# Layer 0's attention mixers hold negated scores: the add-and-minimum of each row chunk gives the exponential's bias

## The chip, the cores and the metric

The kernel runs on one core of a Trainium2 chip. The metric is the time of one execution on the device in microseconds (us), the median over several runs; lower is better. A core has TensorE (PE, with the weight loads as PEld), VectorE (DVE), ScalarE (ACT), GpSimd (POOL) and SyncE (SP, which here issues the loads and stores), each with its own queue of instructions.

## The reference

A trunk of two layers over one sequence of 2048 tokens of width 1024, in float32. Layer 0 projects the normalised input once and runs two attention mixers side by side, each with 8 heads of 64 columns; their gated outputs go through one output projection. Layer 1 is a differential attention with its own projections.

```python
def sliding_window_sink_attention(q, k, v, sinks):        # mixer A
    # each chunk of 64 queries sees its own and the 2 chunks before
    scores = jnp.einsum('bcqhgd,bclhd->bchgql', qc, kb) / math.sqrt(HEAD_DIM)
    scores = jnp.where(valid, scores, NEG_INF)
    probs = jax.nn.softmax(jnp.concatenate([scores, sink], axis=-1), axis=-1)[..., :-1]
    out = jnp.einsum('bchgql,bclhd->bcqhgd', probs, vb)
...
def chunked_relbias_attention(q, k, v, rel_table):        # mixer B
    # each chunk of 64 queries sees its own and the 8 chunks before
    scores = jnp.einsum('bcqhd,bclhd->bhcql', qc, kb) / math.sqrt(HEAD_DIM)
    scores = scores + bias[None, :, None, :, :]           # learned, by clipped distance
    probs = jax.nn.softmax(jnp.where(valid, scores, NEG_INF), axis=-1)
    out = jnp.einsum('bhcql,bclhd->bcqhd', probs, vb)
```

A softmax is computed as exp(score - m) divided by its row's sum, where m is a number at least near the row's maximum. Mixer A's row has one more entry, the head's learned sink, which counts in the sum alone.

## The kernel before

Layer 0 first projects (names that begin with p0), stores queries, keys, values and gates to memory, and then `_mix0` runs the mixers (names that begin with m). Layer 1 follows (p1, then c).

In `_mix0` the tokens are handled in 4 blocks of 512, from the last block to the first. Each block has 8 A heads and 8 B heads, in pairs: two A heads, two B heads, and so on. A generator `heads` produces the scores of one head after the other (`scores_a`, `scores_b`) and puts its second half (`values_a`, `values_b`: transposes of the probabilities, products with the values, the join) into a queue; `pace` runs that queue 9 units behind the scores and lays the output projection (`mom`) or late gates (`mlg`) beside them. The order in which the instructions then stand on each engine is set by a scheduler when the program is built.

A score tile lies in one of 3 PSUM banks (tag S). One A head has 4 row chunks of 128 queries; two of them share a bank (`mSA`, 128 x 2 x 256). The kernel writes a large negative number over the masked corners (L633, L634; L632 in the first block of tokens), takes the maximum of each row with its sign turned (L635, result `manm`), takes the minimum of that and the negated sink (L637), and gives it to ScalarE as the exponential's bias (L641), which reads the bank and writes the probabilities to `mPA` in SBUF, of which there are 2 buffers. L642 computes the sink's share, L644 and L645 the row sums' reciprocal, and GpSimd multiplies (L647).

One B head has 4 row chunks of up to 640 keys, in two pieces of 384 and 256 (`mSB`), one bank each. L717 adds the mask or bias and takes the maximum in one custom operation, whose result is read by a second instruction (the accumulator read, `mbm`); it writes the sum to `mPB`, of which there are 8 buffers. L719 (or L721, where there is one piece) joins the two maxima and turns the sign (`mbnm`), L723 is the exponential, L724 the reciprocal `mbr` and L725 GpSimd's multiplication.

In the second halves TensorE transposes the probabilities into one of 3 banks (`mtrA` L675, `mtrB` L740), ACT and DVE split the result in a high and a low part (`mptH` L591, `mptL` L592), TensorE multiplies both by the values into one bank (`mOA`, `mOB`; L682, L684, L744, L745), and ACT and DVE join its halves (`mlow` L599, `myt` L600).

## Time and profile before

| | |
|---|---|
| median of 3 runs | 2830.96 us |
| lowest and highest run | 2825.42 and 2834.3 us |
| span of the profiled execution, first to last instruction | 2813.0 us |
| median less that span | 17.96 us |
| instructions | 44676 |
| layer 0's mixers, from the span's start | about 600 to 1130 us |

The profile records the span of one execution; what lies around it is known only as the difference to the median above. A row of the profile has the line of the source, the engine, the operation, what it writes and reads, shapes, the count, the busy time in us and the mean of one in ns, and then the engine's idle time before these instructions with what ended it. Matmuls overlap each other, so their means are longer than their pitch.

### The profile page before, as it was taken

What the parts mean: (1) busy time and instruction counts of PE and PEld (TensorE: products, weight loads), DVE (VectorE), ACT (ScalarE), POOL (GpSimd) and SP (SyncE); (2) the same over time, 40 slices, a digit from 0 to 9 for tenths busy, and PEclk for the clock granted to TensorE, in tenths of its full rate; (3) what the DMA queues carried; (4) which work ended last, traced back from release to release, by engine and by line L of the source; (5) the groups of instructions that cost most, each with busy time, mean ns of one, the idle gap of its engine ahead of it and who ended that gap; (6) DMA issues with size and microseconds to landing.
All of it is one profiled execution on the core that took longest, in us unless ns stands there. A gap on an engine that the chain in (4) does not pass through costs nothing.

```text
span 2813.0 us, 44676 instructions
## 1 busy us (share of the span) xinstructions
PE 2693.0 (96%) x13384; PEld 2164.3 (77%) x13384; DVE 1875.9 (67%) x5073; ACT 1623.8 (58%) x4135; POOL 1458.8 (52%) x1548
## 2 busy tenths in 40 slices
PE   7999999999899999889999999999999999999998
PEld 5888888888788888777788888776676777677776
DVE  7752285347788886598807880468786788777762
ACT  5443543267767675343435331578897787777761
POOL 3541252234645354266845660457676666767761
PEclk9999999999999999999999999999999999999999
DMA  5673343739977765565885444787868675455542
GB/s 174 223 244 138 109 142 121 221 111 240 234 191 189 199 186 140 184 239 194 252 268 187 128 142 142 238 253 208 238 199 234 181 215 186 140 175 152 168 148 85
DMA packets 356098, 521.73 MB, mean 185 GB/s; under 512 B 44816, under 2 KB 139792, under 8 KB 355856
## 3 DMA queue, kind: packets, MB, share of 16 engines
q1 hardware_dynamic: 355856, 518.87, 62.2%
q8 instruction: 107, 1.75, 0.3%
q14 instruction: 135, 1.11, 0.1%
HBM read 361.70 MB, written 157.02 MB: 184 GB/s over the span
## 4 chain that ended last, share of the span: by engine, by line
PE 72%; DVE 11%; DMA 8%; ACT 4%; issue 3%; POOL 1%; SPq 0%; DVEq 0%; ACTq 0%; POOLq 0%
PE cO L968 7%; PE p1mm L213 5%; PE p1mm L214 5%; PE p1mm L215 5%; PE cS L913 4%; PE cS L914 4%; PE ctr L964 3%; PE p0mm L213 3%; PE p0mm L214 3%; PE p0mm L215 3%; PE com L213 2%; PE com L214 2%; PE com L215 2%; PE mom L213 2%; PE mom L215 2%
## 5 line engine op out<-in xcount | busy, mean ns | idle before, releaser
L920 ACT ACTIVATE cP<-cS,cnm 128x512 f32<-128x512 f32 (+3 forms) x640 | 394.2, 622 | 121.7 <-DVE cnm L917 104.0
L917 DVE TENSOR_REDUCE cnm<-cS 128x1 f32<-128x512 f32 (+3 forms) x640 | 374.5, 601 | 52.9 <-PE cS L914 46.0
L952 POOL TENSOR_TENSOR cP<-cP,cP 128x512 f32<-128x512 f32 (+1 forms) x320 | 353.0, 1131 | 37.7 <-ACT cP L950 37.4
L951 POOL TENSOR_SCALAR cP<-cP,crl,cel 128x512 f32<-128x512 f32 (+3 forms) x288 | 209.4, 740 | 234.2 <-DVE crl L933 113.6
L213 PE MATMUL p1mm<-p1wH,p1hH 128*128 128x512 f32 x768 | 303.6, 396 | 5.5 <-ACT p1wH L308 5.5
L215 PE MATMUL p1mm<-p1wH,p1hL 128*128 128x512 f32 x768 | 304.0, 396 | 0.0
L214 PE MATMUL p1mm<-p1wL,p1hH 128*128 128x512 f32 x768 | 303.5, 396 | 0.1
L310 POOL TENSOR_TENSOR p0wL<-p0ws,p0wH 128x512 fp32r<-128x512 f32 (+1 forms) x124 | 149.8, 1237 | 265.6 <-ACT p0wH L308 255.2
L968 PE MATMUL cO<-cpt,cv 128*128 128x512 f32 (+3 forms) x640 | 285.4, 531 | 1.4 <-DVE cpt L966 1.3
L913 PE MATMUL cS<-ck,cqd 128*128 128x512 f32 (+3 forms) x640 | 264.2, 416 | 12.2 <-ACT cP L920 11.6
L966 DVE COPY cpt<-ctr 128x512 f32<-128x512 f32 (+1 forms) x320 | 191.4, 606 | 105.0 <-PE ctr L964 101.1
L213 PE MATMUL p0mm<-p0wH,p0hH 128*128 128x512 f32 (+1 forms) x640 | 238.4, 374 | 7.1 <-ACT p0vt L472 4.8
L215 PE MATMUL p0mm<-p0wH,p0hL 128*128 128x512 f32 (+1 forms) x640 | 238.4, 373 | 2.5 <-DVE p0hL L336 2.4
L214 PE MATMUL p0mm<-p0wL,p0hH 128*128 128x512 f32 (+1 forms) x640 | 238.6, 373 | 0.0
L310 POOL TENSOR_TENSOR p1wL<-p1ws,p1wH 128x512 fp32r<-128x512 f32 x128 | 167.8, 1331 | 127.9 <-ACT p1wH L308 121.3
L914 PE MATMUL cS<-ck,cql 128*128 128x512 f32 (+3 forms) x640 | 231.8, 366 | 0.0
L964 PEld LDWEIGHTS ctr<-ident,cP 128*128 128x128 f32 x1088 | 137.0, 141 | 115.4 <-issue 60.8
L950 ACT ACTIVATE cP<-cP,cc 128x512 f32<-128x512 f32 (+3 forms) x288 | 172.2, 662 | 15.7 <-DVE cc L948 15.3
L964 PE MATMUL ctr<-ident,cP 128*128 128x128 f32 x1088 | 175.2, 273 | 2.7 <-POOL cP L952 2.7
L213 PEld LDWEIGHTS p1mm<-p1wH,p1hH 128*128 128x128 f32 x768 | 145.7, 190 | 34.5 <-ACT p1wH L308 5.7
L214 PEld LDWEIGHTS p1mm<-p1wL,p1hH 128*128 128x128 f32 x768 | 145.5, 190 | 29.5 <-POOL p1wL L310 0.9
L215 PEld LDWEIGHTS p1mm<-p1wH,p1hL 128*128 128x128 f32 x768 | 145.4, 189 | 28.9
(303 smaller groups left out, 7115.9 us busy)
## 6 DMA issues: line engine op xcount, KB each, us to landing
p1ws<-in_od_w_in_dram SPq DMA_DIRECT2D x56, 512.0 KB, 4.2
p0ws<-in_ev_w_in_dram SPq DMA_DIRECT2D x48, 512.0 KB, 4.4
ck<-kH SPq DMA_DIRECT2D x144, 128.0 KB, 3.5
ck<-kL SPq DMA_DIRECT2D x144, 128.0 KB, 3.7
cv<-v SPq DMA_DIRECT2D x72, 256.0 KB, 4.2
cqd<-qH SPq DMA_DIRECT2D x128, 128.0 KB, 4.8
cql<-qL SPq DMA_DIRECT2D x128, 128.0 KB, 4.8
cwH<-wgH SPq DMA_DIRECT2D x64, 256.0 KB, 4.7
```

The costliest lines, as they stand in the source:

```text
L213: mm(ps, aH, bH, start=first, stop=False)
L214: mm(ps, aH, bL, start=False, stop=False)
L215: mm(ps, aL, bH, start=False, stop=last)
L310: low.tensor_tensor(l[:, :width], ws[:, k, :width], f32(h[:, :width]), ALU.subtract)
L913: mm(ps, qd[:, m, js], kt[:, :wd], start=True, stop=False)
L914: self.anchor = mm(ps, ql[:, m, js], kt[:, :wd], start=False, stop=True).ins
L917: nc.vector.tensor_reduce(nm[:, m, z:z + 1], ps, AX.X, ALU.max, negate=True)
L920: exp = nc.scalar.activation(chunks[z][:, :wd], ps, AF.Exp, bias=nm[:, m, z:z + 1], accum_out=acc).ins
L951: nc.gpsimd.tensor_scalar(p1, p1, rl[:, 0:1], e1, ALU.mult, ALU.mult)
L952: nc.gpsimd.tensor_tensor(p1, p1, p2, ALU.add)
L964: nc.tensor.transpose(tp[:, (j - j0) * P:(j - j0 + 1) * P], us[j][kt // 4][:, kk:kk + P], self.ident)
L968: mm(O[:, j0 * P:], v, T[:, :wd], start=(kt == 0), stop=(kt == nkt - 1), skip_group_check=True)
```

## The change

The query's scale is negative in layer 0 (`-0.125` in A's rotary table and in B's gain), so every score arrives negated, and the exponential is taken with scale -1 and the row's minimum as bias.

In mixer A the two memsets, the maximum and the sink's minimum are replaced by one custom operation for each row chunk (L636): it adds a mask tile `mwin` to the negated scores, writes the sum to `mPA`, and takes the minimum over the row, which starts from the negated sink. Its accumulator read gives `manm`. The exponential then works in place on `mPA` in SBUF. In the first block of tokens the half of the first row chunk that is masked as a whole is left out.

In mixer B the custom operation (L722) takes the minimum; the second piece of a row chunk starts from the first one's result, so the step that joined the two is gone. The reciprocal (L728) is taken for two row chunks at a time, and GpSimd's multiplications (L731) of the two follow it. `far` is no longer negated beforehand. The mask tile takes memory, and the scratch that the program keeps for DMA descriptors is made smaller (16384 to 1024 bytes of a partition).

```diff
+POS = -NEG
...
-        nc.vector.scalar_tensor_tensor(self.b_gain, gq, 0.125, gk, ALU.mult, ALU.mult)
+        nc.vector.scalar_tensor_tensor(self.b_gain, gq, -0.125, gk, ALU.mult, ALU.mult)
...
-                tabs["q"] = self.rope_tables(tb, self.gain[gq], 0.125, n + "tq")
+                tabs["q"] = self.rope_tables(tb, self.gain[gq], 0.125 if layer else -0.125, n + "tq")
...
+        win = ld.tile([P, 256], F32, tag="win", name=n + "win", bufs=1)
+        nc.gpsimd.memset(win, 0.0)
+        nc.gpsimd.memset(win[0:HD, 192:256], POS)
+        nc.gpsimd.memset(win[HD:P, 0:64], POS)
         nc.sync.dma_start(far, a["relfar"].to_broadcast([P, 8]))
-        nc.vector.tensor_scalar(far, far, -1.0, None, ALU.mult)
...
+            lows = [P if b * NTB + j == 0 else 0 for j in range(NTB)]
             for z in range(2):
...
-                if b == 0 and z == 0:
-                    nc.vector.memset(ps[:, 0, 0:P], NEG)
-                nc.vector.memset(ps[0:HD, :, 192:256], NEG)
-                nc.vector.memset(ps[HD:P, :, 0:64], NEG)
-                nc.vector.tensor_reduce(nm[:, zs], ps, AX.X, ALU.max, negate=True)
-                for j in (2 * z, 2 * z + 1):
-                    nc.vector.tensor_scalar(nm[:, j:j + 1], nm[:, j:j + 1], self.nsink[:, h:h + 1], None, ALU.min)
+                for i in range(2):
+                    j, lo = 2 * z + i, lows[2 * z + i]
+                    nc.vector.tensor_tensor_reduce(
+                        pt[:, j, lo:], ps[:, i, lo:], win[:, lo:], 1.0, self.nsink[:, h:h + 1], ALU.add, ALU.min, nm[:, j:j + 1]
+                    )
                 yield 1
                 for i in range(2):
-                    j = 2 * z + i
-                    nc.scalar.activation(pt[:, j, :], ps[:, i, :], AF.Exp, bias=nm[:, j:j + 1], accum_out=l[:, j:j + 1])
+                    j, lo = 2 * z + i, lows[2 * z + i]
+                    nc.scalar.activation(
+                        pt[:, j, lo:], pt[:, j, lo:], AF.Exp, bias=nm[:, j:j + 1], scale=-1.0, accum_out=l[:, j:j + 1]
+                    )
...
-            nc.gpsimd.tensor_scalar(bias, bias, 1.0, far[:, h:h + 1], ALU.mult, ALU.add)
-            nc.gpsimd.memset(bias[0:HD, 192:256], NEG)
+            nc.gpsimd.tensor_scalar(bias, bias, -1.0, far[:, h:h + 1], ALU.mult, ALU.add)
+            nc.gpsimd.memset(bias[0:HD, 192:256], POS)
+            l, r = small("bl", 4), small("br", 4)
...
-                    nc.vector.tensor_tensor_reduce(pb[:, ca:cz], ps, by, 1.0, NEG, ALU.add, ALU.max, m[:, z:z + 1])
-                if len(cuts) == 2:
-                    nc.vector.tensor_scalar(nm, m[:, 0:1], m[:, 1:2], -1.0, ALU.max, ALU.mult)
-                else:
-                    nc.vector.tensor_scalar(nm, m[:, 0:1], -1.0, None, ALU.mult)
+                    least = m[:, 0:1] if z else POS
+                    nc.vector.tensor_tensor_reduce(pb[:, ca:cz], ps, by, 1.0, least, ALU.add, ALU.min, m[:, z:z + 1])
                 yield 7 / 8
-                nc.scalar.activation(pb[:, w0:640], pb[:, w0:640], AF.Exp, bias=nm, accum_out=l)
-                nc.vector.reciprocal(r, l)
-                nc.gpsimd.tensor_scalar(pb[:, w0:640], pb[:, w0:640], r, 1.0, ALU.mult, ALU.mult)
+                nc.scalar.activation(
+                    pb[:, w0:640], pb[:, w0:640], AF.Exp, bias=m[:, z:z + 1], scale=-1.0, accum_out=l[:, j:j + 1]
+                )
+                if j % 2:
+                    nc.vector.reciprocal(r[:, j - 1:j + 1], l[:, j - 1:j + 1])
+                    for i in (j - 1, j):
+                        pi, wi = (probs[-1], max(0, 5 - t) * P) if i < j else (pb, w0)
+                        nc.gpsimd.tensor_scalar(pi[:, wi:640], pi[:, wi:640], r[:, i:i + 1], 1.0, ALU.mult, ALU.mult)
...
-    nc = bacc.Bacc("TRN2", target_bir_lowering=False, num_devices=1)
+    nc = bacc.Bacc("TRN2", target_bir_lowering=False, num_devices=1, dynamic_dma_scratch_size=1024)
```

The scheduler orders the instructions anew from the mixers' first score on. Up to there the order is the same, and so it is again in all of layer 1's mixer; in between each engine's order differs in many places.

On DVE, in the first block handled, where an A head's last scores and the next B head's first ones meet (ISA is the custom operation or its accumulator read), there stood before:

```order
L634 MEMSET mSA 64x2x64
L592 TENSOR_TENSOR mptL<-mtrB,mptH 128x128
L635 TENSOR_REDUCE manm<-mSA 128x2
L592 TENSOR_TENSOR mptL<-mtrB,mptH 128x384
L717 ISA mPB,mbm<-mSB,medge 128x384
L717 ISA mbm 128x1
L637 TENSOR_SCALAR manm<-manm,nsink 128x1 x2
L717 ISA mPB,mbm<-mSB,mbias 128x256
L717 ISA mbm 128x1
L592 TENSOR_TENSOR mptL<-mtrB,mptH 128x256
L592 TENSOR_TENSOR mptL<-mtrB,mptH 128x128
L719 TENSOR_SCALAR mbnm<-mbm 128x1
```

On DVE at the same place there stands now:

```order
L596 TENSOR_TENSOR mptL<-mtrB,mptH 128x256
L596 TENSOR_TENSOR mptL<-mtrB,mptH 128x128
L636 ISA mPA,manm<-mSA,mwin,nsink 128x256
L636 ISA manm 128x1
L636 ISA mPA,manm<-mSA,mwin,nsink 128x256
L636 ISA manm 128x1
L722 ISA mPB,mbm<-mSB,medge 128x384
L722 ISA mbm 128x1
L596 TENSOR_TENSOR mptL<-mtrB,mptH 128x384
L722 ISA mPB,mbm<-mSB,mbias,mbm 128x256
L722 ISA mbm 128x1
```

A bank of mixer A is done after two operations and their reads, which now write `mPA`; the splits that lay between the steps of the maximum stand ahead of them or behind; mixer B's second operation reads the first one's result.

On TensorE, in the second block handled, from the last transpose of an A head whose `mPA` the second A head of the next pair uses, there stood before:

```order
L675 MATMUL mtrA<-ident,mPA 128x128
L215 MATMUL mom<-mw,myL 128x512
L585 MATMUL mSB<-mks,mqd 128x384
L586 MATMUL mSB<-mks,mql 128x384
L740 MATMUL mtrB<-ident,mPB 128x128 x8
L682 MATMUL mOA<-mptH,mvA 128x128
L684 MATMUL mOA<-mptL,mvA 128x128
```

On TensorE at the same place there stands now:

```order
L678 MATMUL mtrA<-ident,mPA 128x128
L215 MATMUL mom<-mw,myH 128x512
L216 MATMUL mom<-mw,myL 128x512
L214 MATMUL mom<-mw,myH 128x512
L215 MATMUL mom<-mw,myH 128x512
L216 MATMUL mom<-mw,myL 128x512
L589 MATMUL mSB<-mks,mqd 128x384
L590 MATMUL mSB<-mks,mql 128x384
L746 MATMUL mtrB<-ident,mPB 128x128 x4
L589 MATMUL mSB<-mks,mqd 128x256
L590 MATMUL mSB<-mks,mql 128x256
L214 MATMUL mom<-mw,myH 128x512
```

The B head's second score (128x256) needs the bank that the A head's first two minimums free, and these wait for the transpose at the top; more of the output projection moved in between.

On TensorE, at such a transpose in the first block handled, there stood before:

```order
L675 MATMUL mtrA<-ident,mPA 128x128
L585 MATMUL mSB<-mks,mqd 128x384
L586 MATMUL mSB<-mks,mql 128x384
L740 MATMUL mtrB<-ident,mPB 128x128 x8
L585 MATMUL mSB<-mks,mqd 128x256
L586 MATMUL mSB<-mks,mql 128x256
L213 MATMUL mlg<-p0hH,p0wH 128x512
```

On TensorE at the same transpose there stands now:

```order
L678 MATMUL mtrA<-ident,mPA 128x128
L216 MATMUL mlg<-p0hH,p0wL 128x512
L589 MATMUL mSB<-mks,mqd 128x384
L590 MATMUL mSB<-mks,mql 128x384
L746 MATMUL mtrB<-ident,mPB 128x128 x4
L589 MATMUL mSB<-mks,mqd 128x256
L590 MATMUL mSB<-mks,mql 128x256
L589 MATMUL mSB<-mks,mqd 128x384
L590 MATMUL mSB<-mks,mql 128x384
L746 MATMUL mtrB<-ident,mPB 128x128 x4
```

Here two scores follow one another closely behind the transpose, each in a bank that two of the A head's minimums free.

More of the change, by code (lines that the diff above doesn't have):

```diff
@@ L564, in _mix0 @@
         nc.gpsimd.memset(edge, 0.0)
-        nc.gpsimd.memset(edge[HD:P, 0:64], NEG)
+        nc.gpsimd.memset(edge[HD:P, 0:64], POS)
+        win = ld.tile([P, 256], F32, tag="win", name=n + "win", bufs=1)
+        nc.gpsimd.memset(win, 0.0)
+        nc.gpsimd.memset(win[0:HD, 192:256], POS)
+        nc.gpsimd.memset(win[HD:P, 0:64], POS)
         nc.sync.dma_start(far, a["relfar"].to_broadcast([P, 8]))
-        nc.vector.tensor_scalar(far, far, -1.0, None, ALU.mult)
         group = {}
@@ L622, in scores_a @@
             pt = sb.tile([P, NTB, 256], F32, tag="PA", name=n + "PA")
+            lows = [P if b * NTB + j == 0 else 0 for j in range(NTB)]
             for z in range(2):
-                zs = slice(2 * z, 2 * z + 2)
                 ps = pS.tile([P, 2, 256], F32, tag="S", name=n + "SA")
@@ L628, in scores_a @@
                     c0 = (b * NTB + j - 1) * P - k0
-                    lo = P if c0 < 0 else 0
-                    score(ps[:, i, lo:256], res["q"], j, ks, c0 + lo, c0 + 256)
-                if b == 0 and z == 0:
-                    nc.vector.memset(ps[:, 0, 0:P], NEG)
-                nc.vector.memset(ps[0:HD, :, 192:256], NEG)
-                nc.vector.memset(ps[HD:P, :, 0:64], NEG)
-                nc.vector.tensor_reduce(nm[:, zs], ps, AX.X, ALU.max, negate=True)
-                for j in (2 * z, 2 * z + 1):
-                    nc.vector.tensor_scalar(nm[:, j:j + 1], nm[:, j:j + 1], self.nsink[:, h:h + 1], None, ALU.min)
+                    score(ps[:, i, lows[j]:256], res["q"], j, ks, c0 + lows[j], c0 + 256)
+                for i in range(2):
[3 more added lines that the diff above has]
+                    )
                 yield 1
                 for i in range(2):
-                    j = 2 * z + i
-                    nc.scalar.activation(pt[:, j, :], ps[:, i, :], AF.Exp, bias=nm[:, j:j + 1], accum_out=l[:, j:j + 1])
+                    j, lo = 2 * z + i, lows[2 * z + i]
+                    nc.scalar.activation(
+                        pt[:, j, lo:], pt[:, j, lo:], AF.Exp, bias=nm[:, j:j + 1], scale=-1.0, accum_out=l[:, j:j + 1]
+                    )
             nc.scalar.activation(es_, nm, AF.Exp, bias=self.sink[:, h:h + 1])
@@ L646, in scores_a @@
             for j in range(NTB):
-                nc.gpsimd.tensor_scalar(pt[:, j, :], pt[:, j, :], r[:, j:j + 1], 1.0, ALU.mult, ALU.mult)
+                nc.gpsimd.tensor_scalar(pt[:, j, lows[j]:], pt[:, j, lows[j]:], r[:, j:j + 1], 1.0, ALU.mult, ALU.mult)
             res.update(p=pt, v=vt, k0=k0)
@@ L711, in scores_b @@
                 cuts = [(w0, 384), (384, 640)] if w0 < 384 else [(w0, 640)]
-                m, nm, l, r = small("bm", 2), small("bnm"), small("bl"), small("br")
+                m = small("bm", 2)
                 for z, (ca, cz) in enumerate(cuts):
```

## The prediction

> **What bounds the kernel now.** I read the page first, then a table of stretches, then what TensorE waits for in the stretch that the change touches, then the groups of instructions with shapes apart.
>
> ```profile
> span 2813.0 us, 44676 instructions
> PE 2693.0 (96%) x13384; PEld 2164.3 (77%) x13384; DVE 1875.9 (67%) x5073; ACT 1623.8 (58%) x4135; POOL 1458.8 (52%) x1548
> PE 72%; DVE 11%; DMA 8%; ACT 4%; issue 3%; POOL 1%; SPq 0%; DVEq 0%; ACTq 0%; POOLq 0%
> ```
>
> TensorE is busy for 96% of the span and carries 72% of the chain that ended last; DVE is the next owner with 11%. No TensorE instruction is removed, so only TensorE's idle time can be won. The stretches, in microseconds from the span's start, say how much of it lies where layer 0's two mixers run:
>
> ```profile
> core 0: us, PE busy (x) PEld busy (x) DVE busy (x) ACT busy (x) POOL busy (x), PEclk, DMA share, GB/s
> 540.00:600.00 60.00, 58.75 (x257) 47.68 (x256) 7.16 (x11) 21.00 (x35) 13.31 (x14) 1.00 0.51 151
> 600.00:1130.00 530.00, 496.61 (x3097) 437.63 (x3096) 412.14 (x1529) 369.07 (x987) 259.36 (x389) 0.99 0.74 192
> 1130.00:1200.00 70.00, 61.84 (x287) 50.53 (x286) 39.78 (x73) 25.29 (x58) 15.52 (x11) 0.95 0.65 207
> 1200.00:2813.00 1613.00, 1563.10 (x7175) 1198.39 (x7174) 1109.21 (x2781) 971.11 (x2504) 977.41 (x950) 0.99 0.63 190
> ```
>
> The mixers of layer 0 fill 600 to 1130: 530 us, of which TensorE is idle for 530.00 - 496.61 = 33.4. DVE is busy for 412 of them (78%), and the DMA engines for 74%. After 1200 layer 1 runs; the order of its mixer is not changed on any engine, so I leave it at its time. What ends TensorE's idle time in 600 to 1130, in total, times and longest:
>
> ```profile
> PE mtrB L740 <- DVE mptL L592: 8.8, 13, 2.2
> PE mOB L744 <- DVE myt L600: 4.7, 10, 0.8
> PE mSA L585 <- ACT mPA L641: 3.0, 2, 2.2
> PE mSB L586 <- DMA mql<-bqL: 3.0, 3, 1.3
> PE mSB L585 <- ACT mPA L641: 2.9, 6, 1.0
> PE mom L215 <- POOL myL L612: 2.5, 1, 2.5
> PE mSB L585 <- DVE mbm L717: 2.0, 3, 0.7
> PE mSB L585 <- ACT maes L642: 1.6, 1, 1.6
> PE mOA L682 <- DVE myt L600: 1.3, 2, 0.9
> PE mtrA L675 <- DVE mptL L592: 1.1, 2, 0.8
> ```
>
> Two kinds matter. A score that waits for mixer A's exponential (L641, L642) waits for a score bank: 3.0 + 2.9 + 1.6 = 7.5 us. A wait for DVE is one for a split, a join or a minimum that stood in DVE's queue: 8.8 + 4.7 + 2.0 + 1.3 + 1.1 = 17.9 us. DMA (3.0) and GpSimd (2.5) own the rest. A third loss sits inside the busy time:
>
> ```profile
> 698.73:702.14 3.41, 3.41 (x13) 2.99 (x12) 2.56 (x13) 1.62 (x4) 0.00 (x0) 0.51 1.04 208
> 733.00:736.27 3.27, 1.38 (x5) 0.64 (x5) 2.20 (x5) 3.22 (x9) 3.27 (x7) 0.99 0.80 110
> 736.27:739.68 3.41, 3.02 (x10) 2.62 (x10) 2.48 (x9) 2.98 (x8) 3.41 (x7) 0.51 1.01 355
> 770.41:773.82 3.41, 3.41 (x15) 3.08 (x15) 3.29 (x8) 2.15 (x5) 2.57 (x7) 0.51 0.85 215
> 896.70:900.11 3.41, 1.06 (x7) 0.51 (x4) 3.38 (x8) 3.08 (x11) 2.47 (x3) 0.99 1.04 274
> 900.11:903.52 3.41, 3.37 (x17) 3.37 (x18) 1.93 (x6) 3.02 (x12) 1.95 (x5) 0.51 1.06 237
> ```
>
> The columns are those above. When TensorE was busy for only 1.38 or 1.06 us of some 3.3, the next 3.41 us ran at half the granted clock, which costs about 3.41/2 = 1.7 us. With the windows from 698.73 and 770.41 there are four in this stretch, 6.8 us. The Trainium skill, "TensorE: Matmul & The Clock Gate", section "HAM oscillation — how this bites in real kernels", gives the rule as no idle gaps above about 3.4 us; by it, stalls of at most 2.5 us would leave the clock alone and this term would be zero. The trace disagrees, and the trace decides.
>
> **The change part by part.** The rows that price it:
>
> ```profile
> L641 ACT ACTIVATE mPA<-mSA,manm 128x256 f32<-128x256 f32 x128 | 59.6, 475 | 20.3 <-DVE manm L637 18.6 <-PE mSA L586 1.3 <-PE mlg L215 0.2
> L641 ACT ACTIVATION_READ_ACCUMULATOR mPA<-mSA,manm 128x1 f32 x128 | 26.4, 206 | 0.0
> L717 DVE CUSTOM_DVE_ANT_0 mPB<-mSB,mbias 128x256 f32<-128x256 f32 x120 | 50.1, 417 | 7.9 <-PE mSB L586 5.0 <-PE mtrB L740 2.3
> L717 DVE DVE_READ_ACCUMULATOR2_ANT mbm<- 128x1 f32 x240 | 19.7, 82 | 0.0
> L635 DVE TENSOR_REDUCE manm<-mSA 128x2 f32<-128x512 f32 x64 | 43.0, 676 | 0.8
> L633 DVE MEMSET mSA<- 64x128 f32 x64 | 10.5, 165 | 11.0 <-PE mSA L586 6.6
> L634 DVE MEMSET mSA<- 64x128 f32 x64 | 10.5, 165 | 5.9
> L637 DVE TENSOR_SCALAR manm<-manm,nsink 128x1 f32<-128x1 f32 x128 | 18.9, 193 | 0.2
> L719 DVE TENSOR_SCALAR mbnm<-mbm 128x1 f32<-128x1 f32 x112 | 22.8, 205 | 0.1
> L721 DVE TENSOR_SCALAR mbnm<-mbm 128x1 f32<-128x1 f32 x16 | 2.4, 148 | 0.2
> L724 DVE RECIPROCAL mbr<-mbl 128x1 f32<-128x1 f32 x128 | 20.4, 159 | 18.1 <-ACT mPB L723 16.2 <-POOL mPB L725 0.9
> L723 ACT ACTIVATE mPB<-mPB,mbnm 128x256 f32<-128x256 f32 x8 | 4.0, 502 | 2.0 <-DVE mbnm L721 1.2 <-POOL myt L605 0.8
> ```
>
> Mixer A, DVE. Out go the memsets, the maximum and the sink's minimum: 10.5 + 10.5 + 43.0 + 18.9 = 82.9 us. In come 128 add-and-minimums of 128x256 with their accumulator reads, the form of L717: 128 x (417 + 82) = 63.9 us. Their first value is a column in memory, where L717 has a constant. No row prices that; the nearest is a one-column operation with a column operand (L719, 205 ns) against one without (L721, 148), 57 ns, so 128 x 57 = 7.3 us, between 0 and 128 x 205 = 26.2. Net -11.7.
>
> Mixer B, DVE. Out go the negated maxima, 22.8 + 2.4 = 25.2 us, and half of the reciprocals, since one of two columns serves two chunks: 10.2. The second minimum now takes the first one's result as a column: 112 x 57 = 6.4 us, and waits for it; the bounds are 0 and 112 x 205 = 23.0. Net -29.0. Together DVE gets 40.7 us lighter, 412 to 371, with bounds of -54 and -5 (both columns at 0 and at 205 ns).
>
> That does not itself move the end. I turn it into waits by DVE's free time: 530 - 412 = 118 us before and 159 after. The load over the free time falls from 3.5 to 2.3, by a third, and I let the 17.9 us of waits for DVE fall as much: -6.0. Bounds 0 (the waits are dependencies through ACT and not queueing) and -17.9.
>
> Mixer A's score banks. A bank is free today after memsets, maximum and sink's minimums (2 x 165 + 676 + 2 x 193 = 1392 ns) and two exponentials (2 x 475 = 950), at least 2.3 us; after the change the exponential reads memory and the bank is free after two minimums, 2 x 499 = 1.0 us. I keep 43% of the 7.5 us: -4.3. Bounds 0 and -7.5.
>
> The clock. Two of the four half-speed windows should go with the shorter stalls: -3.4. Bounds 0 and -6.8.
>
> The exponential of A, ACT. It reads SBUF in place of PSUM: 502 ns against 475, 128 x 27 = 3.5 us on an engine that is busy for 369 of 530 us and that TensorE waits for through the banks, which are now free before it: 0. The Trainium skill, "Perfetto Trace Analysis", section "Optimizing Scalar/DVE Operations", speaks against this move: about 93 ns of access per ScalarE instruction on SBUF against 51 on PSUM. By it 128 x 42 = 5.4 us is my estimate, hidden in the same place; the row's smaller difference is used.
>
> Normalisation of B in pairs, GpSimd. The same multiplications, the even one a chunk later, the odd one behind it. GpSimd is busy for 259 of 530 us, and TensorE waits for no normalisation in the list above: 0. If that cover failed, it would be one multiplication per pair. The masks (two more memsets and a tile, once), the negated far bias, the signs in the rotary tables and the gain, and the first block's half-width tiles are single instructions before 600 or shorter ones off the path: 0. The smaller DMA scratch only frees memory; every load is issued by SP in both: 0.
>
> **The new wait.** Mixer A's minimum now writes the probability tile, of which there are two, so it must wait until TensorE has transposed the head two before. Today only the exponential writes there. One second head of a pair:
>
> ```profile
> 724.66 0.69 DVE L635 TENSOR_REDUCE manm<-mSA 128x2 f32<-128x512 f32 x1
> 727.76 0.28 PE L675 MATMUL mtrA<-ident,mPA 128*128 128x128 f32 x1
> ```
>
> The maximum ran at 724.66, and the last transpose of the tile that its head will use ended at 728.04: a minimum in its place would have stood for 3.4 us, and behind it in DVE's queue the splits and joins that TensorE needs. The order of the changed kernel shows what TensorE has to do meanwhile. In the second block, 11 TensorE instructions lie between that transpose and the first score that needs the freed bank, and 16 before the next one; at 496.61/3097 = 0.160 us each that is 1.8 and 2.6 us, against 1.0 and 2.0 us for two and four minimums. There it is covered. In the first block handled one pair has 7 and 9 of them: 1.1 and 1.4 us against 1.0 and 2.0, a wait of 0.56 us. Counted in the same way over all pairs of the changed order, seven second heads have 4 to 7 and 9 to 11 instructions, and the rest have about enough; 7 x 0.56 = 3.9 us of new wait. Bounds 0 and the first rival's price.
>
> The sum: -6.0 - 4.3 - 3.4 + 3.9 = -9.8 us, a span of 2803.2. The median of the three runs, 2830.96, lies 17.96 above the profiled span; I take that as what lies around the span and unchanged, so 2830.96 - 9.8 = 2821.2, stated as 2821.
>
> **The rivals.**
> First, slower: the new wait decides. Sixteen pairs of A heads run, and 14 or 15 second heads reuse a tile that was busy late; I count 14. If half of the 3.4 us reached TensorE at each, that is 14 x 1.7 = 24 us in place of 3.9, and with the gains of 13.7 the time is 2830.96 + 10.3 = 2841. It decides from 13.7/14 = 0.98 us per pair. For it: the row at 724.66, and that DVE's queue is strict. Against it: the order puts some of TensorE's other work behind the transpose at every pair.
> Second, the same: what goes from DVE comes back as another wait. The DMA engines are at 1.01 to 1.06 in the windows above, so heads that finish sooner may only wait for their loads, which the waits for mql (3.0) already show; and the DVE waits may be chains through ACT. Then the banks and the new wait alone count, -4.3 + 3.9, and the time is 2831.
> Third, the change does more: all three terms at their bounds, -17.9 - 7.5 - 6.8 = -32, which gives 2799. Against it: a join costs its chain through ACT however free DVE is.
>
> **How the numbers follow.** A change of 0.3%, 8.5 us, is about what a measurement of this kernel tells from none. The forecast gets 0.52, and since its sum of 9.8 is only just beyond that bound, 0.37 of it lies on the faster side and 0.15 on the side of no change; its own range is 2812 to 2828. The third rival has 0.09, the second 0.26 and the first 0.13. That makes 0.46 for faster, 0.41 for no change and 0.13 for slower. The range for 8 in 10 takes in the second rival and reaches into the first and the third: 2804 to 2838.
>
> **What would show it.** Between 600 and the end of the mixers, TensorE's idle time falls from 33 to some 27 us and DVE's busy time by about 41; the scores' waits for L641's successor vanish and a smaller one for the minimum stands in their place; half-speed windows fall from four to two; layer 1's length stays. The forecast is wrong if DVE shows idle time at A's minimum that ends with a transpose and TensorE's waits for splits and joins grow with it, or if waits for loads take over.

## The result, and the profile after

| | before | after |
|---|---|---|
| median of 15 runs each | 2826.11 us | 2814.32 us |
| lowest and highest run | 2819.56 and 2834.3 us | 2810.95 and 2825.77 us |
| ratio of after to before, 95% interval | | 0.9965 [0.9953, 0.9976] |
| span of the profiled execution | 2813.0 us | 2810.4 us |

The ratio is worth 2826.11 x 0.0035 = 9.9 us (the medians themselves lie 11.8 apart); 9.8 had been forecast. In the last group of experiments the same pair gave 0.9961 [0.9947, 0.9975], 11 us. The page of after, the lines that answer to the first ones of before:

```profile
span 2810.4 us, 44478 instructions
PE 2699.2 (96%) x13384; PEld 2168.2 (77%) x13384; DVE 1838.0 (65%) x4808; ACT 1629.7 (58%) x4135; POOL 1456.0 (52%) x1551
PE 77%; DVE 8%; DMA 7%; ACT 3%; issue 2%; POOL 1%; SPq 1%; DVEq 0%; ACTq 0%; POOLq 0%
```

DVE's share of the chain fell from 11% to 8%, TensorE's rose to 77%. The spans differ by only 2.6 us, far less than the medians: the execution of before that was profiled was a short one, and one execution cannot carry the comparison. So I cut both kernels from A's first score to layer 1's first transposes, the stretch that the change touches, and use two executions of each: of before the first profile and that of a kernel with the same order of instructions (the first experiment below), of after the first profile and a repeat. The columns are those of the stretches in the prediction. Before, twice:

```profile
600.70:1148.10 547.40, 511.50 (x3161) 449.58 (x3160) 418.76 (x1547) 374.01 (x999) 259.95 (x389) 0.99 0.75 194
```

```profile
596.30:1149.60 553.30, 515.97 (x3161) 453.02 (x3160) 421.59 (x1547) 373.75 (x999) 260.08 (x389) 0.98 0.74 192
```

After, twice:

```profile
595.90:1139.10 543.20, 514.05 (x3162) 449.52 (x3161) 385.32 (x1283) 377.90 (x999) 259.32 (x389) 0.98 0.71 195
```

```profile
600.10:1139.60 539.50, 509.28 (x3161) 446.34 (x3160) 386.15 (x1283) 377.94 (x999) 259.37 (x389) 0.99 0.71 197
```

The stretch is 550.4 us on average before and 541.4 after, 9.0 less, beside the 9.9 of the ratio. TensorE's idle time (length less the first busy column) was 35.9 and 37.3, and is 29.2 and 30.2; its busy time, with the same matmuls, was 511.5 and 516.0 and is 514.1 and 509.3. What follows the stretch lasted 1664.9 and 1674.7 us before, 1671.3 and 1682.7 after (span less the stretch's end). These lie 18 us apart for a layer whose mixer stands in one order, and they do not follow the kernel: in the experiments below, too, they run from 1668.6 to 1681.2. So I take them as differences between executions, and not as the change's. What TensorE waits for after, between 600 and 1130:

```profile
PE mtrB L746 <- DVE mptL L596: 12.9, 26, 1.6
PE mOB L750 <- DVE myt L604: 5.3, 13, 0.8
PE mSB L589 <- DVE manm L636: 1.9, 4, 0.7
PE mSB L590 <- DMA mql<-bqL: 1.2, 2, 1.0
PE mtrA L678 <- DVE mptL L596: 0.7, 1, 0.7
```

The scores' waits for A's exponential (7.5 us) are gone, with 1.9 us for the new minimum in their place; the waits of B's scores for the maximum that frees their bank (L717, 2.0) are gone too. The waits for splits did not shrink as forecast but grew, from 8.8 to 12.9. The rows that price the new instructions, shapes apart:

```profile
L722 DVE CUSTOM_DVE_ANT_0 mPB<-mSB,mbias,mbm 128x256 f32<-128x256 f32 x112 | 53.4, 477 | 4.3 <-PE mSB L590 2.5
L636 DVE CUSTOM_DVE_ANT_0 mPA<-mSA,mwin,nsink 128x256 f32<-128x256 f32 x120 | 52.3, 479 | 13.1 <-PE mtrA L678 5.6 <-PE mSA L590 3.4 <-DMA g<-p0gt 2.3
L728 DVE RECIPROCAL mbr<-mbl 128x2 f32<-128x2 f32 x64 | 10.4, 162 | 13.5 <-ACT mPB L724 12.8
L642 ACT ACTIVATE mPA<-mPA,manm 128x256 f32<-128x256 f32 x120 | 59.6, 499 | 6.6 <-DVE manm L636 6.4
```

And what DVE waits for in the stretch: one row of before (its first profile), then two of after.

```profile
DVE mptL L592 <- ACT mptH L591: 21.4, 36, 4.4
```

```profile
DVE mptL L596 <- ACT mptH L595: 38.8, 46, 4.4
DVE mPA L636 <- PE mtrA L678: 6.2, 6, 2.1
```

The last row is the new wait: six times A's minimum stood until TensorE had transposed the head two before. The rows above it fit the splits that did not come sooner: DVE waited 21.4 us for ScalarE's half of a split in the first profile of before (24.2 in the second), and waits 38.8 (36.9) now. A lighter DVE that arrives earlier and waits for ScalarE would look like this; that ScalarE is not later instead was not tested.

### The profile page after: what moved, and what is told of

Its sections match the earlier page's. It is cut to its first block, busy times and chain, and to the rows that moved or that the text cites. A ratio compares the mean times of both kernels' runs of the same rounds, so it can differ in the third digit from the quotient of the medians.

```text
span 2810.4 us, 44478 instructions
## 1 busy us (share of the span) xinstructions
PE 2699.2 (96%) x13384; PEld 2168.2 (77%) x13384; DVE 1838.0 (65%) x4808; ACT 1629.7 (58%) x4135; POOL 1456.0 (52%) x1551
## 4 chain that ended last, share of the span: by engine, by line
PE 77%; DVE 8%; DMA 7%; ACT 3%; issue 2%; POOL 1%; SPq 1%; DVEq 0%; ACTq 0%; POOLq 0%
PE cO L974 7%; PE p1mm L216 5%; PE p1mm L214 5%; PE p1mm L215 5%; PE cS L919 4%; PE p0mm L214 4%; PE cS L920 4%; PE p0mm L215 4%; PE p0mm L216 4%; PE ctr L970 3%; PE com L214 2%; PE mom L214 2%; PE com L215 2%; PE com L216 2%; PE mom L215 2%
## 5 line engine op out<-in xcount | busy, mean ns | idle before, releaser
L958 POOL TENSOR_TENSOR cP<-cP,cP 128x512 f32<-128x512 f32 (+1 forms) x320 | 353.0, 1130 | 38.0 <-ACT cP L956 37.6
L215 PEld LDWEIGHTS p1mm<-p1wL,p1hH 128*128 128x128 f32 x768 | 146.0, 190 | 29.9 <-POOL p1wL L311 0.9
```

The source lines that it names most:

```text
L215: mm(ps, aH, bL, start=False, stop=False)
L958: nc.gpsimd.tensor_tensor(p1, p1, p2, ALU.add)
```

## Experiments

Each kernel was timed beside the kernel before on its chip; the three groups of four ran on three chips. All changed kernels but the first are ordered anew by the scheduler, so that an edit is never quite alone; where that weakens a reading I say so. The stretch is that of the tables above, of one execution each; half-speed windows are of 3.41 us, inside it.

| kernel | ratio to before, 95% | stretch, us | TensorE idle | half-speed windows |
|---|---|---|---|---|
| before | 1 | 547.4 | 35.9 | 4 |
| same order, smaller scratch | 1.0000 [0.9983, 1.0017] | 553.3 | 37.3 | 7 |
| A alone | 1.0025 [1.0009, 1.0042] | 558.9 | 36.9 | 9 |
| A alone, three mPA | 0.9993 [0.9977, 1.0009] | 551.2 | 37.4 | 6 |
| B: pairs of reciprocals alone | 0.9995 [0.9978, 1.0012] | 552.1 | 37.1 | 7 |
| B: chained minimum alone | 0.9966 [0.9946, 0.9986] | 544.0 | 35.2 | 4 |
| B alone | 0.9948 [0.9930, 0.9965] | 542.7 | 32.2 | 4 |
| B alone, again | 0.9960 [0.9945, 0.9975] | 541.4 | 30.5 | 4 |
| after | 0.9965 [0.9953, 0.9976] | 543.2 | 29.2 | 5 |
| after, again | 0.9961 [0.9947, 0.9975] | 539.5 | 30.2 | 2 |
| after, three mPA | 0.9946 [0.9926, 0.9966] | 542.0 | 29.9 | 5 |
| after, work added in the projection | 0.9988 [0.9970, 1.0006] | 544.8 | 32.6 | 3 |
| after, work added behind A's minima | 1.0032 [1.0014, 1.0050] | 560.9 | 41.9 | 7 |
| after, A's banks held longer | 0.9993 [0.9981, 1.0006] | 549.8 | 35.9 | 8 |

**The scratch size alone.** The kernel before with the last line of the diff.

```
-    nc = bacc.Bacc("TRN2", target_bir_lowering=False, num_devices=1)
+    nc = bacc.Bacc("TRN2", target_bir_lowering=False, num_devices=1, dynamic_dma_scratch_size=1024)
```

> The kernel before with only the smaller DMA scratch (1024 bytes of a partition); every engine's order is that of the kernel before. Theory (the gain of 10 us comes from layer 0's mixers): no difference, ratio to the kernel before 0.999 to 1.001. Rival (the scratch or another placement in memory brings the gain): 0.9965. Its profile is also a second look at the old order: if the mixers' stretch, from the first score of mixer A to the first transpose of layer 1's projection, is again 547 us, executions of one program agree there; if it is 550 or more, the first profile was a fast execution.

2826.48 us, ratio 1.0000 [0.9983, 1.0017]: the scratch is worth nothing that can be measured. Since every engine's order is that of before, its profile also served as a second one of before, and it showed how far executions of one order differ: 11.3 us in the span, 5.9 in the stretch (547.4 and 553.3), so that the first one was a fast one, as the expectation had it for 550 or more.

**Mixer A's part alone.** A's lines of the diff (win, the add-and-minimum, the exponential on mPA, the half-width tiles and the sign of the query's table); B as before.

> Mixer A changed, mixer B as before (its gain positive, maxima joined, one reciprocal for each chunk). Theory (TensorE's waits for score banks held by mixer A's exponential went away, 7.5 us to about 2): most of the gain, -5 to -8 us, ratio 0.997 to 0.998, with no wait of a score for L642 in the list. Rival (a lighter DVE is what counts, and B sheds 29 of the 41 us): -3 us, 0.999. Rival (the new order as a whole is luck): any value, and the parts don't add up.

2835.53 us, ratio 1.0025 [1.0009, 1.0042]: slower, where the theory and the rival of the lighter DVE both had a gain. The stretch, what TensorE waited for in it, and DVE's row for the new wait:

```profile
598.60:1157.50 558.90, 522.05 (x3162) 455.32 (x3161) 402.67 (x1475) 379.14 (x999) 259.44 (x389) 0.97 0.73 190
```

```profile
PE mSB L590 <- DVE manm L637: 6.7, 6, 3.2
PE mSB L591 <- DMA mql<-bqL: 6.2, 4, 4.4
PE mSB L590 <- DMA mqd<-bqH: 2.3, 2, 2.1
```

```profile
DVE mPA L637 <- PE mtrA L679: 7.3, 9, 1.8
```

DVE is busy for 16 to 19 us less (402.7 against 418.8 and 421.6), and TensorE idles as long as before, 36.9 us. The waits for banks that the exponential held are gone; the minimum's own (6.7) and those for queries (6.2 + 2.3) have their place, in stalls of up to 4.4 us. What is longer in this execution is TensorE's busy time (522.05 against 511.5 and 516.0), with nine half-speed windows. It was a long execution of its kernel (2840.6 us), so the trace does not say how the 8 us of the medians come about.

**Mixer B's part alone.** B's lines of the diff (the chained minimum, the sign of the gain, the bias and the edge, reciprocals in pairs); A as before.

> Mixer B changed, mixer A as before. Theory of the banks: the scores' waits for A's exponential stay at 6 to 9 us, and the gain is small, 0 to -3 us, ratio 0.999 to 1.000. Rival (lighter DVE): -7 us, 0.9975.

2813.11 us, ratio 0.9948 [0.9930, 0.9965]: all of the gain, and more than either expectation had. A's banks are held as before, and that still shows:

```profile
596.50:1139.20 542.70, 510.54 (x3161) 448.28 (x3160) 405.66 (x1354) 375.21 (x999) 260.28 (x389) 0.99 0.71 195
```

```profile
PE mtrB L743 <- DVE mptL L592: 8.1, 14, 2.8
PE mSB L585 <- ACT mPA L641: 4.8, 7, 1.7
PE mSA L585 <- ACT mPA L641: 2.4, 2, 2.2
```

Against the two profiles of before, the waits of B's scores for the maximum went from 2.0 and 2.0 to 0.8, those of the output projection for GpSimd (L612) from 2.5 and 2.7 to nothing, and those for queries from 3.0 and 5.7 to 1.1 + 1.1 = 2.2. So only 1.2 us of the gain lie in scores' waits for the operation that B's part changes.

DVE's busy column is only 13 to 16 us lower, less than with A alone. This does not show that B's part takes less off DVE, since the column counts overlapping records once (in the first execution of before the records add up to 503.9 us, where it has 418.8). By its own rows B's part sheds 22.8 + 2.4 us of joins and 20.4 - 10.4 of reciprocals and adds 112 x 60 ns = 6.7, which is 28.5 less; A's part sheds 19.6, as worked out below. After these two runs the amount of DVE's work and its place are both still possible. The parts could also simply add up: 1.0025 x 0.9948 = 0.9973 lies inside the interval of the whole change.

**A third buffer for mPA in the changed kernel.**

```
-            pt = sb.tile([P, NTB, 256], F32, tag="PA", name=n + "PA")
+            pt = sb.tile([P, NTB, 256], F32, tag="PA", name=n + "PA", bufs=3)
```

> The changed kernel with three buffers of mPA in place of two, so that mixer A's minimum need not wait for the transposes of the head two before. Theory (the new wait costs a few us of TensorE, 1.9 shown as waits for the minimum and part of the grown waits for splits): 2 to 5 us faster than the changed kernel, ratio 0.995 to 0.996 to the kernel before, and DVE's idle time at the minimum that ends with a transpose (6.2 us) gone. Rival (that wait is covered): as the changed kernel, 0.9965.

2813.59 us, ratio 0.9946 [0.9926, 0.9966]. DVE's wait for the transposes of `mtrA` is gone from its list, and the time is that of B alone. The ratios of this kernel and of the whole change differ by 2826 x 0.0019 = 5 us, and their intervals overlap, so the new wait may cost some us in the whole change, or nothing. TensorE's list has one long row beside this:

```profile
PE mSB L590 <- DMA mql<-bqL: 6.5, 5, 2.5
```

Waits for queries of 6.5 us, more than in either profile of before, thus stand in a kernel that is as fast as any here.

**A third buffer with A alone.** The same line in the kernel with A's part alone.

> The kernel before with the change made in mixer A alone, and a third buffer for A's probabilities mPA. Theory W (A alone is slower because its minimum, which now writes mPA, waits for the transposes that last read that buffer: 7.3 us of waits of DVE in the run of A alone, and 7.1 us of TensorE behind it): the wait goes, and with it most of the 8 us; 2822 to 2829, ratio 0.998 to 1.001. Rival L (A's loss comes from its longer instructions on ScalarE and DVE, and from the order that the scheduler makes of them): 2832 to 2838, ratio 1.002 to 1.004.

2827.25 us, ratio 0.9993 [0.9977, 1.0009], as theory W had it: without the wait for the transposes A alone costs nothing that can be measured, and brings nothing either. The stretch, and what TensorE's list has now:

```profile
602.80:1154.00 551.20, 513.79 (x3162) 451.14 (x3161) 400.92 (x1475) 379.68 (x999) 259.33 (x389) 0.98 0.73 193
```

```profile
PE mSB L591 <- DMA mql<-bqL: 7.3, 5, 3.6
PE mSA L591 <- DMA mql<-aqL: 4.1, 1, 4.1
PE mSB L590 <- DMA mqd<-bqH: 1.5, 1, 1.5
PE mSB L590 <- DVE manm L637: 0.2, 1, 0.2
```

The minimum's 6.7 us are down to 0.2, and the waits for queries stand at 7.3 + 4.1 + 1.5 = 12.9 us, against 3.0 in the first profile of before and 5.7 in the second. TensorE's idle time is the same with two buffers and with three (36.9 and 37.4 us); the shorter stretch lies in its busy time (522.05 and 513.79), with six half-speed windows in place of nine. The two kernels with A alone ran on different chips, each beside the kernel before. That the waits for queries took what the lighter DVE could have brought fits these rows; the kernel above, fast with 6.5 us of them, speaks against it, and no run tested it.

**Work added to DVE, at a place that the scheduler chose.** After, with a reduction of a constant table per score bank of A.

```
+                nc.vector.tensor_reduce(small("load"), edge, AX.X, ALU.min)
```

> The changed kernel with one more reduction of a 128x384 table on DVE behind A's minima of each score bank (64 of them, results unused): it puts some 25 to 30 us back on DVE, and leaves all waits and buffers as they are. Theory D (the prediction's first term: TensorE's waits for DVE shrink with DVE's work): the gain shrinks by two thirds; 2820 to 2826, ratio 0.998 to 1.000. Rival C (what counts is the work between a score and its exponential in B, not DVE's sum; a lighter DVE is worth nothing): 2812 to 2817, ratio 0.995 to 0.997.

This did not test what it should: nothing ties the reduction to the scores, and the scheduler put all 64 (0.55 us each) into the projection, where DVE has room.

```profile
L639 DVE TENSOR_REDUCE mload<-medge 128x1 f32<-128x384 f32 x64 | 30.0, 546 | 3.2 <-POOL medge L566 3.2
```

Yet the median was 2825.72 us, ratio 0.9988 [0.9970, 1.0006]: most of the gain was missing, though the order on TensorE, DVE and GpSimd is otherwise that of the changed kernel and ScalarE's differs by one exchange, and the profile's stretch (544.8 us, idle 32.6) looks like it. The profiled execution, 2816.1 us, was the shortest of the twelve, so the trace doesn't show what the others met. The changed kernel itself wasn't timed on that chip, and the two intervals share 0.9970 to 0.9976. I leave this open; it is a warning for each reading here that rests on some 0.3% and one run.

**Halves of B's part.** The first keeps the chained minimum and takes one reciprocal and one normalisation per chunk, as before; the second is the kernel before with the reciprocals in pairs. Of each edit the lines that tell it are shown; the first also has B's signs and masks turned.

```
+                    least = m[:, 0:1] if z else POS
+                    nc.vector.tensor_tensor_reduce(pb[:, ca:cz], ps, by, 1.0, least, ALU.add, ALU.min, m[:, z:z + 1])
...
+                nc.vector.reciprocal(r[:, j:j + 1], l[:, j:j + 1])
```

> The kernel before with the chained minimum in mixer B alone (the joining operation of each chunk falls away); one reciprocal and one normalisation per chunk, as before. Theory C (the joining operation, 112 of 205 ns between a score and its exponential, is what B's gain comes from): 2812 to 2818, ratio 0.994 to 0.997. Rival P (the gain comes from reciprocals in pairs, which halve the places at which DVE waits for an exponential, 33 before and 17 with B changed): 2824 to 2829, ratio 0.999 to 1.001.

```
+                if j % 2:
+                    nc.vector.reciprocal(r[:, j - 1:j + 1], l[:, j - 1:j + 1])
...
```

> The kernel before with only the reciprocals in pairs: one reciprocal and two normalisations per two chunks of mixer B, 32 reciprocals of 128x2 in place of 64 of 128x1 in each half of the mixer; maximum and joining operation as before. Theory C (the joining operation brings B's gain): no change, 2823 to 2829, ratio 0.999 to 1.001. Rival P (the pairs bring it): 2812 to 2818, ratio 0.994 to 0.997.

The chain gave 2817.95 us, 0.9966 [0.9946, 0.9986]; the pairs 2826.32 us, 0.9995 [0.9978, 1.0012]. Theory C, for the larger part: taking the joining operation away and chaining the minimum is a gain by itself, and the pairs alone are none that can be measured. Whether the pairs add something once the join is gone (0.9948 and 0.9960 against 0.9966) the intervals don't say. The stretch of the chain, then of the pairs:

```profile
598.20:1142.20 544.00, 508.81 (x3162) 446.94 (x3161) 409.25 (x1419) 373.94 (x999) 259.98 (x389) 0.99 0.72 195
```

```profile
599.00:1151.10 552.10, 514.99 (x3162) 452.28 (x3161) 414.43 (x1483) 374.24 (x999) 259.62 (x389) 0.98 0.73 192
```

The profile of the chain does not show by which wait the gain comes. TensorE idles for 35.2 us there, nearly as before, and the shorter stretch lies in its busy time, 508.8 against 511.5 and 516.0, in which the half-speed windows count. That the chained minimum without the joining operation is the larger part of the gain is shown by this one run; how it reaches TensorE is not shown.

**The changed kernel and B alone, side by side.**

> The changed kernel once more, on the chip of the three runs beside it, for a second profile and as their measure: ratio 0.995 to 0.998 as at first. In its profile the mixers, from the first score of A to layer 1's first transposes, take 541 to 547 us (543.2 in the first one), with TensorE idle for 28 to 31 us; half-speed windows there may be anything from 3 to 8, if they are an execution's and not a kernel's.

2814.01 us, ratio 0.9961 [0.9947, 0.9975]. Its stretch stands above: 539.5 us, just below the 541 to 547 expected, and two half-speed windows in place of five, by the same code. The forecast of 3 to 8 was too narrow.

> Mixer B's part of the change alone, again, beside the whole change on the same chip. Theory W (in the whole change A's minimum waits for the transposes of mPA's last reader, and so takes back what A's lighter DVE gives): B alone is as short as the whole change or up to 5 us shorter, ratio 0.993 to 0.997. Rival S (the parts add up, and A's part brings its share of the gain with B's in place): B alone is 3 to 6 us longer than the whole change, ratio 0.997 to 0.9985.

2814.51 us, 0.9960 [0.9945, 0.9975], 0.5 us from the whole change. Rival S, by which A's part has a share of the gain once B's is there, would have it 3 to 6 us longer. In the whole change A's part is worth nothing that can be measured; by the two intervals it could still be some 0.002 either way.

**Work added to DVE behind A's minima.** The added operation takes the minimum as its first value, which keeps it there.

```
+                junk = sb.tile([P, 384], F32, tag="junk", name=n + "junk", bufs=1)
+                nc.vector.tensor_tensor_reduce(
+                    junk, edge, edge, 1.0, nm[:, 2 * z:2 * z + 1], ALU.add, ALU.min, small("load")
+                )
```

> The changed kernel with one more add-and-minimum of the 128x384 table with itself on DVE behind the minima of each of A's 64 score banks, which takes the minimum as its first value, so that it stays among the mixers' work (in the run with the independent reduction the scheduler put all 64 into the projection); 64 x (0.52 + 0.08) = 39 us more of DVE, its results unused. Theory D (TensorE's waits shrink and grow with DVE's work): the whole gain goes, 2822 to 2832, ratio 0.998 to 1.002, with TensorE's idle time in the mixers back at 34 to 38 us. Rival C (what counts is the joining operation between a score and its exponential in B): 2812 to 2818, ratio 0.995 to 0.9975, idle time at 28 to 31.

2835.10 us, ratio 1.0032 [1.0014, 1.0050], 21 us more than the changed kernel beside it. Rival C, by which only B's joining operation counts, is out: DVE's work at this place counts. Theory D has the direction, and the size was too small (2822 to 2832, idle time of 34 to 38). The row of the added operation, and the stretch:

```profile
L640 DVE CUSTOM_DVE_ANT_0 mjunk<-medge,manm 128x384 f32<-128x384 f32 x64 | 54.4, 849 | 0.1
```

```profile
597.70:1158.60 560.90, 519.05 (x3161) 450.92 (x3160) 427.80 (x1411) 378.28 (x999) 266.10 (x389) 0.98 0.72 189
```

```profile
PE mtrB L750 <- DVE mptL L596: 11.1, 27, 1.8
PE mOA L691 <- DVE mptL L596: 5.1, 1, 5.1
PE mSB L590 <- DMA mql<-bqL: 4.6, 5, 2.1
PE mSB L589 <- DVE manm L636: 4.1, 6, 1.5
```

One added operation took 849 ns, not the 520 that the expectation had, and with the accumulator reads (5.0 us) 54.4 + 5.0 = 59.4 us were put on, not 39. Theory D's 8 to 18 us over the changed kernel, enlarged as 59 to 39, are 12 to 27, and 21 lies inside. DVE's busy column is at 427.8 us, only 6 to 9 above before, and TensorE idles for 41.9. The waits of B's transposes for splits are not longer than after (11.1 against 12.9); the idle time came as one stall of 5.1, as waits for A's minimum and as waits for queries.

**A's banks held as before.** After, with a copy of one column of each bank on ScalarE behind A's exponentials.

```
+                nc.scalar.activation(small("hold"), ps[:, 1, 255:256], AF.Copy)
```

> The changed kernel with a copy of one column of each of A's 64 score banks on ScalarE behind the exponentials that once read the bank, so that the bank is held as long as before the change (64 small copies on ScalarE more, which lengthen the hold by about 0.2 us each). By the prediction's second term (4.3 us for banks held by A's exponentials): 2817 to 2821, ratio 0.9965 to 0.9985, with waits of scores for ScalarE of 6 to 10 us in the profile. Rival (the waits for banks only moved to the splits, which grew from 9.9 to 13.8 us): no change against the changed kernel, within 2 us of it, and the waits for splits back at 9 to 11.

2824.83 us, ratio 0.9993 [0.9981, 1.0006], 10.8 us more than the changed kernel beside it. Both expectations missed the time: the prediction's term had said 4.3, the rival nothing. The rival's other sign, waits for splits back at 9 to 11, is there with 9.7.

```profile
598.70:1148.50 549.80, 513.91 (x3161) 452.60 (x3160) 386.75 (x1283) 380.69 (x1063) 258.90 (x389) 0.98 0.73 194
```

```profile
PE mSB L590 <- DMA mql<-bqL: 6.6, 4, 2.7
PE mSB L589 <- DMA mqd<-bqH: 2.1, 1, 2.1
PE mSA L589 <- ACT mhold L645: 1.7, 1, 1.7
PE mSB L589 <- ACT mhold L645: 1.5, 2, 1.2
```

The waits for banks are back with 3.2 us only; the waits for queries have grown from 1.2 and 2.4 to 8.7, and there are eight half-speed windows. DVE still waits for the transposes, but no wait for the minimum is left in TensorE's list:

```profile
DVE mPA L636 <- PE mtrA L679: 5.9, 9, 1.5
```

A bank that is held longer thus goes with the loss of B's gain. Whether A's part needs the early bank to come out even is a reading and not shown: how much of the 10.8 us is the longer hold and how much the other order that the scheduler then makes was not separated.

## Why the prediction was right, and where it was not

The sum, -9.8 us, was right: 9.9 and 11 were measured. Between 600 and 1130 TensorE's idle time went from 33.4 us to 530.00 - 501.54 = 28.5, where 27 was forecast. Which waits went, the terms had largely wrong, so that the sum came out is in good part luck. One of the prediction's own signs of being wrong even came true: DVE stood idle at A's minimum until a transpose (6.2 us), and TensorE's waits for splits grew with it (8.8 to 12.9).

**What lies around the span, 17.96 us.** Mis-sized, though it cancels in the forecast. Each execution's own time of these two kernels is 1.7 to 1.9 us above its span (2812.16 against 2810.4 for after). The rest of the 17.96 is that the profiled execution, at some 2813.0 + 1.8 = 2814.8 us, was shorter than any timed one of the kernel before (2817.72 at the least), and the median of three far above it. That median was also 4.9 us above that of fifteen. The forecast of 2821, taken from it, lies 6.9 above the 2814.3 measured: 4.9 of that is the median of three, and 2.0 that the medians differ by 11.8 and not 9.8. Every "before" of the prediction (33.4 us idle, four half-speed windows) came from that short execution.

**Waits for DVE, -6.0.** This step failed as a sum of waits. The rows that stood at 17.9 us stand at 12.9 + 5.3 + 0.7 and a few tenths, 19 us. Its lower bound, "dependencies through ACT", fits the row of 38.8 us. DVE's busy time fell by 33 to 36 us in the stretch, not 40.7. The prediction took sums of rows off that column, but removed records had overlapped others. A's sum of 82.9 also mixes the two: the row of L637 has 18.9 us of busy time, where its 128 records of 193 ns are 24.7, and L632 (1.3) is not in it. By the records' own durations 10.5 + 10.5 + 1.3 + 43.3 + 24.7 = 90.3 us went from A, and 120 x 479 ns + 8 x 345 + 128 x 82 = 70.7 came in, 19.6 less and not 11.7. B's 28.5 agrees with the 29.0.

The law behind the term, waits in proportion to load over free time, is not borne out by the rows of waits. In the time, though, a microsecond of DVE's rows went with a like price in three places: 25.2 - 6.7 = 18.5 us less for the chain with some 10, 28.5 less for B's part with 11 to 15, 59.4 more behind A's minima with 21, between 0.35 and 0.55 each. A's part falls out, with 19.6 less and nothing gained even with a third buffer. Its place alone does not explain that, since the added operations stood at the same place and cost. Its new wait and the longer waits for queries stand beside it, untested.

**Score banks, -4.3.** The rows agree: 7.5 us of waits for the exponential went (5.2 in the second profile of before), and 1.9 came for the minimum between 600 and 1130, 2.5 in the whole stretch. But they are not a gain of the change that can be added: B alone keeps them (4.8 + 2.4) and is as short. That the early release pays for the new wait would fit the run that held the banks longer; with its other order, that run does not show it.

**The clock, -3.4.** As sized over two executions each (4 and 7 windows before, 5 and 2 after: two fewer on average), but the pair of profiles that I had meant to compare shows four and five, the wrong way round. On the third chip the mean granted clock over all executions was 0.9884 before and 0.9905 after; within one kernel 0.001 of it went with about 2.3 us (2.5 before, 2.2 after), so 0.0021 x 2300 = 4.8 of the 11 to 12 us go with the clock. That is a correlation and not a test.

**The new wait, +3.9.** Shown, at no more than 2.5 us on TensorE and 6.2 on DVE in the whole change, and 7.1 on TensorE with A alone, where it decides: the third buffer takes 1.0025 to 0.9993, on two chips. The first rival's mechanism was real, in A alone; it needed A without B to win.

**The column as first value, 57 ns.** 477 and 479 ns against 417, so 60 to 62. The exponential on SBUF: 499 ns where 502 had been taken; its accumulator read fell from 206 to 189 ns, so that the pair takes 688 ns in place of 681. The reciprocal of two columns: 162 ns against 159.

**The second rival**, gain that comes back as waits for loads, is the nearest to what became of A's part: 12.9 us of waits for queries with A alone and three buffers. With the whole change they fell instead (1.2 and 2.4), so it lost as a forecast; with a third buffer there they stood at 6.5 and cost nothing that shows. Of the windows that it cites for the DMA engines, two of six stand at 0.80 and 0.85, not above 1. That the normalisations in pairs cost nothing that can be measured, and that the scratch does nothing, was right.

What stays open: by which waits the chained minimum shortens TensorE's time, why the waits for queries are short with B's part and long with A's, and whether they cost anything. I tried no kernel with earlier loads.

## What to carry to other kernels

A microsecond taken off an engine that is not the bound has no fixed price. Here taking a short join from between a product of TensorE and its exponential was worth some 10 us, and about as much DVE time taken off the other mixer was worth nothing. A change that lets an instruction write a buffer earlier than its forerunner did takes on that buffer's wait: count the buffers first, and time the parts alone, since here one part had all of the gain and the other none. Before rows of a profile are summed, look whether their records overlap. Before a profile's span is set against a median, compare the span with that execution's own time; with executions 10 to 20 us apart, two profiles of a stretch say more than one of the whole.

## What the hardware showed beside that

The half-speed windows lie on a fixed raster of 3.41 us that does not start with the kernel (an edge of it comes 2.33 us behind the first instruction in the first execution of before, 1.38 us in the second), and short waits are enough for them. After, at the place where TensorE waited 1.6 us for a split (rows from windows of the raster, columns as above):

```profile
887.76:891.17 3.41, 2.75 (x21) 2.38 (x21) 2.26 (x9) 0.16 (x1) 3.41 (x4) 1.00 1.09 338
891.17:894.58 3.41, 1.82 (x14) 1.40 (x13) 1.50 (x3) 3.30 (x10) 3.41 (x7) 0.99 0.98 252
894.58:901.40 6.82, 6.02 (x23) 4.53 (x22) 4.90 (x13) 3.55 (x12) 3.42 (x7) 0.50 0.47 128
```

The same place in the repeat, where the idle time lies across the edge of two windows:

```profile
892.51:895.92 3.41, 2.03 (x11) 1.52 (x11) 2.50 (x9) 2.42 (x7) 3.41 (x6) 1.00 0.84 234
895.92:899.34 3.42, 2.20 (x17) 1.68 (x15) 1.71 (x5) 3.37 (x12) 2.29 (x6) 1.00 0.81 214
899.34:902.75 3.41, 2.86 (x16) 2.38 (x16) 3.35 (x12) 1.68 (x5) 2.05 (x3) 1.00 0.26 93
```

In the first execution TensorE was busy for 1.82 of 3.41 us and then ran at half speed for two windows; in the second a like idle time fell as 1.4 and 1.2 us on two windows, and nothing followed. I put the raster over the stretch in all fourteen traces: behind each of the 47 windows with under 1.5 us of TensorE work the next ran at half speed. Behind windows at full speed with more than 2.06 us none did, and in between both happened. A half-speed window was followed by another where it had up to 2.96 us of work, and by full speed from 3.02. So a stall of 1.4 us can cost 1.7 us for each half-speed window behind it or nothing, by where the raster lies, and executions of one order differ. The Trainium skill, "TensorE: Matmul & The Clock Gate", Part 1 ("The HAM clock gate"), says that the window of 3413 ns is free-running and does not start with the kernel; the traces agree. The same page of the Trainium skill, section "Why this matters for your kernels", advises no idle gaps above about 3 us. That is too mild for a stream like this one: 1.4 to 2 us inside one window were enough here.
